# Other homes for the second branch's turned blocks in a decoder block, and another split of the first branch's transfers over two queues

## The chip, the cores and the metric

The kernel runs on one core of one Trainium2 chip. The metric is the device time of one execution in microseconds (us); before the change the median of three runs is 363.88 us (363.3 to 364.21). Engines are named as in the profile: PE (TensorE), DVE (VectorE), ACT (ScalarE), POOL (GpSimd) and SP (SyncE, which here issues transfers and nothing else). Each engine runs its own instructions in order, and so do the queues into which SP and POOL issue transfers: an instruction that waits holds up all that stand behind it on its engine.

## What is computed

One decoder layer on a sequence of 256 positions with 1024 channels. Two attention branches of 8 heads with 64 channels run side by side on the normalised input; their outputs are gated channel by channel, added and projected, and a gated feed-forward part with a short causal convolution follows. Cut to what matters:

```python
h = rms_norm(x, attn_norm_g)
qa, ka, va, qb, kb, vb, f_logit, g_logit = split(h @ w_in)
qa, ka = partial_rope(rms_norm(heads(qa))), partial_rope(rms_norm(heads(ka)))   # first branch
qb, kb = rms_norm(heads(qb)), rms_norm(heads(kb))                               # second branch
o_a = softmax(mask(qa @ ka.T / 8)) @ va          # one block of 256 keys: causal attention
c   = cumsum(log_sigmoid(f_logit + b_forget))
o_b = softmax(mask(qb @ kb.T / 8 + c[t] - c[s])) @ vb
merged = sigmoid(g0) * (o_a @ w_moba) + sigmoid(g1) * (o_b @ w_fox)
x = x + merged @ w_out
u, g = split(rms_norm(x) @ w_up)
x = x + (silu(conv3(g)) * u) @ w_down
```

All of it is float32 with float32 weights, 66.75 MB of which are read from device memory.

## The kernel before

**Weights.** Every weight chunk is 1 MB (128 x 2048). SP issues its load into one of three buffers "raw" (L132). ACT splits each half into a rounded high part (whi, L141) and DVE into the rest (wlo, L142), six buffers of each; a product is then three matmuls, high by high, high by low and low by high. So every chunk costs two ACT and two DVE instructions, and a raw buffer comes free, and with it the next load, when DVE has taken the second half. The chunks are used in the order of the list `chunks`: q and k of the second branch, `qkv` 1 and 2; gate chunks `wg` 0 and 1; V of the first branch, `qkv` 0 in the halves (0,0) and (0,1); `wg` 2; V of the second branch, `qkv` 3; `wg` 3 to 7; and then the later matrices. q and k of the first branch come with the input in the chunks called "head".

**q and k.** Products of q and k come out with positions on the partitions, and attention wants channels there. `finish_qk` normalises them into qns[0] (tag "qn", first branch) or qns[1] (tag "ol", second branch); in the first branch POOL then applies the rotation in place (L357 to L360). `turn_blocks` (L370) turns them in blocks of 32 x 32 with two DVE transposes of 1024 columns, first the half d=1 and then d=0 (L375), into the tile "pT". `move_blocks` (L380) carries the blocks to their partitions with sixteen transfers of 64 KB (L385), eight on SP for d=1 and eight on POOL for d=0, into the tile "bias". ACT then copies them, scaled, to qTs and kTs (L393 and L396), five instructions in each branch; the second branch's lie in the space "oh".

**Shared space.** "pT" and "bias" have one buffer each, and both branches use them. The second branch's turn into pT therefore waits for the first branch's sixteen transfers out of it, and the second branch's transfers into bias wait for ACT's copies of the first. V (128 x 2 x 1024) is written by `finish_v` (L321, L323) only after the first softmax; "qn" is free from the first branch's turn until the second softmax takes it for two pairs of heads (L497); "bias" becomes the second branch's bias (`forget_bias`, L448), and both pT and bias later take turned probabilities (`turn`, L530).

**Order.** PE's order is the program's. For the other engines a planner picks the order by priorities and expected times, within the orders that `after` writes out by hand. Those that touch this change: SP's transfers of a branch come after a load given as `behind` (L388: `qkv` (0,0) for the first branch, (0,1) for the second); the load of `qkv` (0,1) comes after the first branch's last SP transfer, and that of `wg` 2 after the second's (L134, through `sent_last`); the second branch's turn comes after the split of `wg` 1 (L377, `state["turn"]`); the forget gate's sums (`forget_a`, L408) come after that turn; ACT's split of `qkv` (0,1) comes after its copies of the first branch (L149, `moved[0]`), and the first softmax's exponentials after its copies of the second (L511, `moved[1]`).

PE meanwhile runs: q and k of the second branch, gates 0 and 1, scores of the first branch (L481), V of the first branch (L317), gate 2, scores of the second branch (L481), V of the second branch, gates 3 to 7, and so on.

Of the kernel before, what the change touches and what calls it, by code (L numbers as in the profile page):

```python
# [17 lines left out]
P = 128  # L18
# [26 lines left out]
def decoder_block(ctx, tc, a, out):  # L45
    nc = tc.nc
# [6 lines left out]
    def T(shape, tag, bufs=1, dt=F32):  # L53
        return sb.tile(shape, dt, tag=tag, bufs=bufs, name=tag)
# [4 lines left out]
    def bank():  # L59
        return ps.tile([P, 512], F32, tag="bank", bufs=8, name="bank")  # L60
# [36 lines left out]
    moved = []  # L97
    sent_last = []
# [3 lines left out]
    def after(i, j):  # L102
        tc.add_manual_dep(i.ins, j.ins.name, mybir.DependencyInfo(mybir.DependencyClass.NoSync, mybir.DependencyReason.DATA), reason="order")
# [85 lines left out]
    def col(c, n=1):  # L189
        return sm[:, c:c + n]  # L190
# [104 lines left out]
    V = T([P, NT, 2 * W4], "V")  # L295
# [73 lines left out]

    def turn_blocks(br, behind):  # L370

        blocks = T([P, 3072], "pT")
        for d in (1, 0):
            c = slice(d * 1024, (d + 1) * 1024)
            i = nc.vector.transpose(blocks[:, c], qns[br][:, c])  # L375
            if br or d == 0:
                after(i, behind)  # L377
        return blocks, i

    def move_blocks(br, blocks, behind):  # L380
        moved = T([P, 3072], "bias")
        for d, queue in ((1, nc.sync), (0, nc.gpsimd)):
            for h in range(2):
                for a in range(4):
                    sent = queue.dma_start(moved[64 * h + 32 * d:64 * h + 32 * (d + 1), a * 512:(a + 1) * 512],  # L385
                                           blocks[32 * a:32 * (a + 1), (2 * d + h) * 512:(2 * d + h + 1) * 512])
                    if d:
                        after(sent, behind)  # L388
            if d:
                sent_last.append(sent)  # L390
        v = moved[:, 0:2048].rearrange("p (a s b t i) -> p s t b a i", a=4, s=2, b=4, t=NT)
        q = moved[:, 0:2048].rearrange("p (a s g i) -> p s g a i", a=4, s=2, g=8)[:, 0]
        i = nc.scalar.activation(qTs[br].rearrange("p b (t a i) -> p (b t) a i", t=NT, a=4), q, AF.Copy, scale=gq[:, br:br + 1])  # L393
        kT = kTs[br].rearrange("p b (n a i) -> p n b a i", n=4, a=2)
        for t, a, at in ((0, 0, 2), (0, 2, 3), (1, 0, 1), (1, 2, 0)):
            i = nc.scalar.activation(kT[:, at], v[:, 1, t, :, a:a + 2], AF.Copy, scale=col(C_QG + 2 * br + 1))  # L396
        return i
# [230 lines left out]
    for isk in range(2):  # L628
        pt = banks()
        state["lag"] = 2 * isk  # L630
        project(3 + isk, pt, 0)
        project(3 + isk, pt, 1)
        with soon(FIRST):
            finish_qk(1, ((isk, pt),))
            if isk == 0:
                blocks, i = turn_blocks(0, state["qn"])
# [3 lines left out]
    with soon():  # L640
        moved.append(move_blocks(0, blocks, loads["qkv", 0, 0]))
        blocks, i = turn_blocks(1, state["turn"])
        summed = forget_a(i)
        after(state["v_lo"], summed)
# [4 lines left out]
    with soon():  # L649
        sps = scores(0, read)  # L650
        moved.append(move_blocks(1, blocks, loads["qkv", 0, 1]))
        for pair in range(4):
            scaled = softmax(0, pair, sps[pair], read, moved[1])
            if pair == 0:
                done = scaled
# [93 lines left out]
    sp = bank()  # L749
# [141 lines left out]
```

## Time and profile before

| | us |
|---|---|
| median of three runs | 363.88 |
| the profiled execution | 365.09 |
| its span (first to last instruction) | 363.3 |
| PE busy | 353.3 |
| DVE busy | 278.4 |
| ACT busy | 221.8 |
| POOL busy | 47.7 |

The profile is of one execution. Its own time is 1.8 us more than its span; what the kernel's instructions do lies within the span. Lines of the profile's groups read: line, engine, operation, tile written <- tiles read, count, busy time and mean, and the idle time of that engine just before, with what ended it. In lines in order of time the first two numbers are the start and the time taken in us; "x8" is a run of eight instructions; brackets hold the idle time before and what ended it. For a transfer the time is that of its issue on SP or POOL; when its data has landed is told apart.

### The profile page before, as it was taken

How to read it: one execution, taken by the hardware profiler on the slowest of the kernel's cores; microseconds unless marked ns; L12 is line 12 of the kernel's file. 1: busy time of each engine (PE TensorE's matmuls, PEld its weight loads, DVE VectorE, ACT ScalarE, POOL GpSimd, SP SyncE). 2: the span in 40 equal slices, each digit the busy share in tenths (PEclk: the TensorE clock that was granted, in tenths of full speed). 3: DMA queues.
4: the chain of work that ended last, by engine and by line, in shares of the span. 5: the costliest groups of instructions: out<-in, count | busy, mean ns of one | idle time of the engine just before them, and what ended most of it. 6: DMA issues, size and time to landing. Idle time of an engine off the chain costs nothing.

```text
span 363.3 us, 7518 instructions
## 1 busy us (share of the span) xinstructions
PE 353.3 (97%) x3053; PEld 335.9 (92%) x3053; DVE 278.4 (77%) x476; ACT 221.8 (61%) x378; POOL 47.7 (13%) x73
## 2 busy tenths in 40 slices
PE   9999999898889999999999999999999999999995
PEld 5888898697689999999999999999999999999995
DVE  4899997987998457984979876768686866768643
ACT  5859635499993998544778545546455545546420
POOL 2542751360050000000530000000000000000000
PEclk9999999999999999999999999999999999999998
DMA  7976483767238273654545754554554554554003
GB/s 276 403 307 240 130 252 105 248 267 293 108 116 325 75 299 117 234 197 159 225 145 204 231 195 160 227 189 166 226 187 173 221 203 160 219 191 157 3 0 117
DMA packets 13411, 70.39 MB, mean 194 GB/s; under 512 B 2200, under 2 KB 3360, under 8 KB 5952
## 3 DMA queue, kind: packets, MB, share of 16 engines
q1 hardware_dynamic: 12432, 67.67, 51.7%
q0 software_dynamic: 800, 2.24, 1.9%
q8 instruction: 24, 0.39, 0.4%
q14 instruction: 11, 0.09, 0.1%
q10 hardware_dynamic: 144, 0.00, 0.0%
HBM read 66.75 MB, written 1.06 MB: 187 GB/s over the span
## 4 chain that ended last, share of the span: by engine, by line
PE 72%; DVE 9%; ACT 6%; DMA 5%; SPq 3%; issue 2%; POOL 1%; DVEq 0%; ACTq 0%
PE bank L592 13%; PE bank L590 13%; PE bank L591 13%; PE bank L805 6%; PE bank L804 5%; PE bank L803 5%; DVE wlo L142 3%; PE bank L317 3%; ACT whi L141 2%; PE bank L727 2%; PE bank L701 2%; PE bank L729 2%; PE bank L728 2%; PE bank L703 2%; PE bank L702 2%
## 5 line engine op out<-in xcount | busy, mean ns | idle before, releaser
L142 DVE TENSOR_TENSOR wlo<-raw,whi 128x1024 fp32r<-128x1024 f32 x120 | 146.7, 1229 | 46.7 <-ACT whi L141 46.6
L141 ACT ACTIVATE whi<-raw 128x1024 fp32r<-128x1024 f32 x120 | 125.2, 1058 | 63.1 <-PE bank L591 37.1
L592 PE MATMUL bank<-oh,wlo 128*128 128x256 f32 x352 | 96.8, 275 | 0.0
L590 PE MATMUL bank<-oh,whi 128*128 128x256 f32 x352 | 96.8, 275 | 0.0
L591 PE MATMUL bank<-ol,whi 128*128 128x256 f32 x352 | 96.8, 275 | 0.0
L592 PEld LDWEIGHTS bank<-oh,wlo 128*128 128x128 f32 x352 | 66.1, 188 | 0.0
L590 PEld LDWEIGHTS bank<-oh,whi 128*128 128x128 f32 x352 | 66.1, 188 | 0.0
L591 PEld LDWEIGHTS bank<-ol,whi 128*128 128x128 f32 x352 | 66.1, 188 | 0.0
L590 PE MATMUL bank<-xh,whi 128*128 128x256 f32 x128 | 35.7, 279 | 1.5 <-ACT ol L509 1.5
L592 PE MATMUL bank<-xh,wlo 128*128 128x256 f32 x128 | 35.4, 276 | 1.3 <-DVE wlo L142 1.3
L591 PE MATMUL bank<-xl,whi 128*128 128x256 f32 x128 | 35.3, 276 | 0.0
L590 PEld LDWEIGHTS bank<-xh,whi 128*128 128x128 f32 x128 | 24.0, 188 | 2.5 <-ACT ol L509 1.9
L592 PEld LDWEIGHTS bank<-xh,wlo 128*128 128x128 f32 x128 | 24.0, 188 | 1.5 <-DVE wlo L142 1.5
L591 PEld LDWEIGHTS bank<-xl,whi 128*128 128x128 f32 x128 | 24.0, 188 | 0.1
L317 PE MATMUL bank<-wlo,xh 128*128 128x512 f32 x64 | 21.1, 390 | 1.1 <-DVE wlo L142 1.1
L317 PE MATMUL bank<-whi,xh 128*128 128x512 f32 x64 | 21.2, 391 | 0.1
L317 PE MATMUL bank<-whi,xl 128*128 128x512 f32 x64 | 20.9, 388 | 0.0
L770 DVE TENSOR_TENSOR sq<-bank,rs 128x512 f32<-128x512 f32 x22 | 15.1, 691 | 6.6 <-PE bank L592 6.5
L701 PE MATMUL bank<-oh,whi 128*128 128x256 f32 x64 | 17.6, 275 | 0.0
L702 PE MATMUL bank<-ol,whi 128*128 128x256 f32 x64 | 17.6, 275 | 0.0
L703 PE MATMUL bank<-oh,wlo 128*128 128x256 f32 x64 | 17.6, 275 | 0.0
L727 PE MATMUL bank<-xh,whi 128*128 128x256 f32 x64 | 17.6, 275 | 0.0
(196 smaller groups left out, 767.0 us busy)
## 6 DMA issues: line engine op xcount, KB each, us to landing
raw<-in_wu SPq DMA_DIRECT2D x22, 1024.0 KB, 4.8
raw<-in_wd SPq DMA_DIRECT2D x11, 1024.0 KB, 4.8
raw<-in_qkv SPq DMA_DIRECT2D x8, 1024.0 KB, 6.3
raw<-in_wg SPq DMA_DIRECT2D x8, 1024.0 KB, 4.9
raw<-in_wb SPq DMA_DIRECT2D x4, 1024.0 KB, 5.1
raw<-in_wo SPq DMA_DIRECT2D x4, 1024.0 KB, 4.9
raw<-in_head SPq DMA_DIRECT2D x6, 512.0 KB, 6.6
bias<-pT SPq DMA_DIRECT2D x16, 64.0 KB, 3.7
```

What stands on the lines that cost most here:

```text
L141: i = nc.scalar.activation(hi[:, s], raw[:, s], AF.Copy)
L142: d = nc.vector.tensor_tensor(lo[:, s], raw[:, s], hi[:, s].bitcast(F32), op=ALU.subtract)
L317: nc.tensor.matmul(pt[t], lhs[:, k, t * P:(t + 1) * P], rhs[:, c], start=(k == 0 and i == 0), stop=(k == KT - 1 and i == 2))
L590: nc.tensor.matmul(o, wh[:, w], mh[:, k], start=(k == 0 and i == 0), stop=False)
L591: nc.tensor.matmul(o, wh[:, w], ml[:, k], start=False, stop=False)
L592: nc.tensor.matmul(o, wl[:, w], mh[:, k], start=False, stop=(k == KT - 1 and i == 1))
L701: nc.tensor.matmul(o, wh[:, w], oh[:, 4 * br + k], start=(k == 0), stop=False)
L702: nc.tensor.matmul(o, wh[:, w], ol[:, 4 * br + k], start=False, stop=False)
L703: nc.tensor.matmul(o, wl[:, w], oh[:, 4 * br + k], start=False, stop=(k == 3))
L727: nc.tensor.matmul(o, wh[:, w], mh[:, k], start=(k == 0 and i == 0), stop=False)
L803: nc.tensor.matmul(o, wh[:, w], ah, start=(p == 0 and h == 0 and c == 0), stop=False)
L805: nc.tensor.matmul(o, wl[:, w], ah, start=False, stop=(last and h == 1 and d == ds[-1]))
```

## The change

Three things are changed, all within `turn_blocks` and `move_blocks`:

- the second branch's blocks are turned into V's tile, seen as 128 x 2048, instead of into pT;
- they are carried into a tile of the tag "qn" (128 x 2048) instead of "bias";
- the first branch's sixteen transfers are split twelve to four: the eight of d=1 and the four of d=0 with h=0 on SP, the four of d=0 with h=1 on POOL. The second branch's stay eight and eight. What the load of the next chunk is put behind (`sent_last`) is still the branch's last transfer on SP.

```diff
     def turn_blocks(br, behind):
 
-        blocks = T([P, 3072], "pT")
+        blocks = V.rearrange("p t c -> p (t c)") if br else T([P, 3072], "pT")
         for d in (1, 0):
             c = slice(d * 1024, (d + 1) * 1024)
             i = nc.vector.transpose(blocks[:, c], qns[br][:, c])
@@
     def move_blocks(br, blocks, behind):
-        moved = T([P, 3072], "bias")
-        for d, queue in ((1, nc.sync), (0, nc.gpsimd)):
+        moved = T([P, 2048], "qn") if br else T([P, 3072], "bias")
+        for d in (1, 0):
             for h in range(2):
+                sp = d or h < 1 - br
+                queue = nc.sync if sp else nc.gpsimd
                 for a in range(4):
                     sent = queue.dma_start(moved[64 * h + 32 * d:64 * h + 32 * (d + 1), a * 512:(a + 1) * 512],
                                            blocks[32 * a:32 * (a + 1), (2 * d + h) * 512:(2 * d + h + 1) * 512])
-                    if d:
+                    if sp:
                         after(sent, behind)
-            if d:
-                sent_last.append(sent)
+                if sp:
+                    last = sent
+        sent_last.append(last)
```

## The prediction

> **What bounds the kernel now.** I read the page first (busy times, then the slices), then TensorE's waits and time order, then the chain of waits, then the time order of each queue between 40 and 110 us. Busy times, and TensorE's share of 40 equal slices of the span (9 is 90% or more):
>
> ```profile
> PE 353.3 (97%) x3053; PEld 335.9 (92%) x3053; DVE 278.4 (77%) x476; ACT 221.8 (61%) x378; POOL 47.7 (13%) x73
> PE   9999999898889999999999999999999999999995
> ```
>
> TensorE is busy nearly always; what it loses is four stalls in the middle (in brackets, with what ended each; columns are start us, us, what):
>
> ```profile
> 65.68 0.50 PE L317 MATMUL bank<-wlo,xh 128*128 128x512 f32 x1 [1.13 <-DVE wlo L142]
> 84.31 1.31 PE L481 MATMUL bank<-oh 64*64 64x64 f32 x30 [1.12 <-ACT V L321]
> 98.39 0.36 PE L590 MATMUL bank<-xh,whi 128*128 128x256 f32 x1 [1.53 <-ACT ol L509]
> 108.37 0.38 PE L592 MATMUL bank<-xh,wlo 128*128 128x256 f32 x1 [1.31 <-DVE wlo L142]
> ```
>
> They are 5.1 us in all, the most that an edit of this stage can win. After the last, at 108.37 (the twelfth slice), every slice but the final one is full, so a lead won before 108 reaches the end unchanged.
>
> What do they hang on? The chain of waits (start, us, what) has, ahead of the first softmax:
>
> ```profile
> 52.62 6.40 DMA bias<-pT
> ...
> 62.69 1.70 SPq L385
> ...
> 67.69 4.97 DMA raw<-in_wg
> ...
> 72.75 1.06 ACT whi L141
> ```
>
> and ScalarE (ACT), asked for its waits from 72 to 110 us, has one only:
>
> ```profile
> ACT whi L141 <- DMA raw<-in_wg: 0.5, 1, 0.5
> ```
>
> So ScalarE works without a gap from 72.75 to 110, beginning with the split of gate chunk 2. The chunk's load is issued at 67.69, because SP's queue is in order and the eight transfers of the second branch's q and k stand in front of it; these stood waiting for the first branch. VectorE (DVE) has small gaps in 73 to 100 us, each ended by ScalarE. The second, third and fourth stall follow this pair of engines; the first follows VectorE alone.
>
> **The change part by part.**
>
> *Second branch turned into V's space.* VectorE, in time order:
>
> ```profile
> 55.78 1.22 DVE L142 TENSOR_TENSOR wlo<-raw,whi 128x1024 fp32r<-128x1024 f32 x1
> 59.30 2.37 DVE L375 STREAM_TRANSPOSE pT<-ol 128x1024 f32<-128x1024 f32 x2 [2.31 <-DMA bias<-pT]
> 63.36 0.41 DVE L417 TENSOR_TENSOR gates<-gates,rsB 8x256 f32<-8x256 f32 x1
> 63.80 0.69 DVE L600 TENSOR_TENSOR gates<-bank,rsB 128x512 f32<-128x512 f32 x1
> 64.41 3.49 DVE L142 TENSOR_TENSOR wlo<-raw,whi 128x1024 fp32r<-128x1024 f32 x3
> 70.55 0.27 DVE L427 TENSOR_SCALAR gates<-gates 8x256 f32<-8x256 f32 x1
> 73.85 1.23 DVE L142 TENSOR_TENSOR wlo<-raw,whi 128x1024 fp32r<-128x1024 f32 x1 [1.11 <-ACT whi L141]
> ```
>
> The turn waits 2.31 us until the first branch's transfers have left pT. V isn't written before 83.59 (below), so the wait goes: turns from 57.0 to 59.3, the first half done at 58.2. All that follows moves 2.3 up as far as its inputs allow. L417 ends at 61.4; L600 needs the second gate's last product (TensorE goes on to L481 at 61.48, a row below), so it starts at about 61.6 and 0.1 is lost there; the three splits run from 62.2 to 65.7. The first is done at 63.4, and TensorE comes for it at 64.5: the stall of 1.13 goes. L427 comes at 68.3, and VectorE stands at the split of chunk 2, for which it is free at about 72.7 now, at 70.5.
>
> *Second branch carried into qn's space.* SP and GpSimd (POOL) queues:
>
> ```profile
> 44.23 5.83 SPq L385 DMA_DIRECT2D bias<-pT  x8
> 50.16 1.49 SPq L132 DMA_DIRECT2D raw<-in_qkv  x1
> 61.50 6.15 SPq L385 DMA_DIRECT2D bias<-pT  x8
> ```
> ```profile
> 49.13 3.99 POOL L385 DMA_DIRECT2D bias<-pT  x8 [3.14 <-DVE pT L375]
> 62.20 1.47 POOL L385 DMA_DIRECT2D bias<-pT  x3 [9.09 <-DVE gates L414]
> 63.85 2.44 POOL L385 DMA_DIRECT2D bias<-pT  x5 [0.18 <-issue]
> ```
>
> Now SP may begin only when ScalarE has read the first branch out of bias (61.47). In qn's space the last readers are the first branch's turns, over before 49.13, when GpSimd, which waits for them, begins; so SP waits for the first half's turn alone, and begins at 58.2 instead of 61.50. Its eight issues took 6.15, with one of 1.70 among issues of 0.6; without that one, about 5.1. I take 6.15: SP is through at 64.4, the load of chunk 2 is issued there instead of at 67.69, and lands 4.97 later, at 69.4. GpSimd begins some 0.5 after the second turn (62.20 against 61.67), at 59.8, and ends at 63.9, where it ended at 66.3.
>
> ScalarE, in time order:
>
> ```profile
> 58.72 0.91 ACT L396 ACTIVATE kT<-bias,sm 128x256 f32<-128x256 f32 x2 [5.75 <-DMA bias<-pT]
> 60.58 0.89 ACT L396 ACTIVATE kT<-bias,sm 128x256 f32<-128x256 f32 x2
> 61.38 1.99 ACT L141 ACTIVATE whi<-raw 128x1024 fp32r<-128x1024 f32 x2
> 68.73 0.91 ACT L396 ACTIVATE oh<-bias,sm 128x256 f32<-128x256 f32 x2 [3.97 <-DMA bias<-pT]
> 71.82 0.42 ACT L429 ACTIVATE gates<-gates 8x256 f32<-8x256 f32 x1
> 72.75 1.06 ACT L141 ACTIVATE whi<-raw 128x1024 fp32r<-128x1024 f32 x1 [0.52 <-DMA raw<-in_wg]
> 83.59 0.67 ACT L321 ACTIVATE V<-bank,rsw 128x512 f32<-128x512 f32 x1
> ```
>
> It began to read the second branch 1.1 after SP's last issue ended (67.65 to 68.73) and took 2.75. So: 65.5 to 68.2, then L428 and L429, which need L427, to 69.3. Chunk 2 has landed at 69.4; its split starts at 69.5, not 72.75: **3.25 us** earlier. VectorE, free at 70.5, follows when that split is done, at 70.6, not 73.85. Both engines enter the softmax 3.2 ahead with the same work in the same order.
>
> *New waits.* V's first writer (L321, some 80.4 then) waits for sixteen transfers landed by 67: 13 us of cover. The second softmax's writes to qn's space near 100 us wait for reads over at 68. Nothing is late by these.
>
> *First branch, twelve on SP and four on GpSimd.* The chain's 6.40 is GpSimd's last transfer of that branch, issued beside the 1 MB load of 50.16. Four of GpSimd's eight go: its part ends at 51.1 instead of 53.1. SP gets four more, behind its eight that end at 50.06, when the turns are done: 4 x 0.6 = 2.4, up to 3.5 with one slow issue. The load behind them goes out at 52.5 to 53.6 instead of 50.16.
>
> ```profile
> raw<-in_qkv SPq DMA_DIRECT2D x1, 1024.0 KB, 8.4
> bias<-pT SPq DMA_DIRECT2D x16, 64.0 KB, 3.7
> ```
>
> By these rows (KB each, us from issue to landing) that load landed at 58.5 and will at about 59 to 61; it is split from 61.38 now, and its first VectorE half is due at 64.5, so that is covered. The first branch lands at 53.0 + 3.7 = 56.7, not 59.0, and ScalarE has read it by 59.2, not 61.47. TensorE wants it at 61.48:
>
> ```profile
> 61.48 2.41 PE L481 MATMUL bank<-kT,qT 64*64 64x64 f32 x64
> ```
>
> Value: 0 to 0.1 us, since the second branch no longer waits for the first. I take 0. At worst, with the load at 61 and split to 63, still 0; at best 0.1.
>
> **The sum.** TensorE's stalls: the first (1.13) and second (1.12) fall away, 2.25; the third is set by engines 3.2 ahead, so 0.95 of its 1.53 goes; the fourth keeps its length, as TensorE and VectorE are then equally far ahead. Together 3.2 us. The profiled execution took 365.09, of which 363.3 is span: it would take 361.9. Against the median of the runs, 363.88, which I predict: **360.7**. Bounds: below, VectorE's own 2.3 if ScalarE's order gives nothing beyond it; above, 3.6 if SP's slow issue doesn't recur (VectorE then limits), and the 5.1 of all stalls if the planner also reorders.
>
> **A rule against it.** GpSimd's tensor operations can be held by VectorE here:
>
> ```profile
> 38.96 0.46 POOL L358 TENSOR_TENSOR p<-qn,rsn 128x128 f32<-128x128 f32 x1
> 42.57 1.51 POOL L358 TENSOR_TENSOR p<-qn,rsn 128x128 f32<-128x128 f32 x1
> 42.55 1.21 DVE L142 TENSOR_TENSOR wlo<-raw,whi 128x1024 fp32r<-128x1024 f32 x1
> ```
>
> 1.51 instead of 0.46, beside a split of weights. Its transfer issues were not: 0.49 each, beside splits too (3.99 for eight, 2.44 for five). The Trainium skill (SBUF — State Buffer, "SBUF: two separate sides") says that a transfer issued from GpSimd can starve, since VectorE in some modes locks GpSimd out of the port through which it writes descriptors. By that rule the second branch's last issues, now at 62 to 64 with splits from 62.2 to 65.7 beside them, would be held; the rows speak against it. The rival that it gives is the third below.
>
> **The rivals.**
> 1. *One transfer is caught by the load.* The first branch's fifth to eighth GpSimd transfers, issued from 0.5 us before the load's issue ended (51.65), landed late; the last took 6.40. Here the last is issued at 63.4, the load's issue (0.6) ends at 65.0, 1.6 later, which is safe; if SP has no slow issue it ends at 63.9, and the last transfer may land at 68 to 68.5. ScalarE then reads until 70.8, and its split starts at 71.6: 1.2 won, 362.7. Between, 2 won.
> 2. *The planner puts the work elsewhere.* ScalarE's copies of the second branch, or the turns, keep their old place or stand behind something late; only the first stall's 1.1, or nothing, is won, as ScalarE sets the rest: 363.2 (362.8 to 364.2).
> 3. *GpSimd is held by the splits.* From 62.2 the last three issues wait until 65.7 and end at 67.1, in the midst of 1 MB loads; with 6.40 to landing, 73.0 to 73.5, ScalarE has read them at 75.9 rather than 71.47, so its chain is 4.2 later: 368.1. It decides from the point where the last landing passes 69.1, that is an issue after 62.7 that is caught. For it: nothing but the 1.51 above; against it: every issue at 0.49.
> 4. *More than the sum*: all of the third and part of the fourth stall go too, 359.6.
>
> **Chances.** Forecast (360.0 to 361.6) 0.57; rival 1 0.13; rival 2 0.15; rival 3 and other losses 0.08; rival 4 0.07. 0.3% of 363.88 is 1.1 us, about what a measurement of this kernel can tell from no change. Faster by more: 0.57 + 0.07 + 0.11 of rival 1 = 0.75; within: 0.17; slower: 0.08. The range leaves out the far ends: 359.8 to 363.2.
>
> **What would show it.** Right: the turns L375 without a wait behind the split at about 57; SP's second group of L385 from 58.2; the load of chunk 2 issued near 64.4; ScalarE's split of it near 69.5; no stall of L317 and L481, a third of 0.6 and a fourth of about 1.3. Wrong: L375 or L385 still waiting for a transfer or for ScalarE; GpSimd's issues further apart than 0.5; second-branch landings after 67; or VectorE idle before the first softmax; or a stall after 110 us that isn't there now.

## The result, and the profile after

The changed kernel took 361.97 us in the median of its runs (361.6 to 362.1), against 364.04 for the kernel before in the same comparison: a ratio of 0.9945 (95% interval 0.9928 to 0.9962). Two later comparisons gave 0.9958 and 0.9952 (below). So the change gains 1.6 to 2.1 us; the forecast was 3.2, and 360.0 to 361.6 as the range of its main case. The profiled execution took 361.60, of which 359.8 is span.

Lines from `move_blocks` on are numbered 2 or 3 higher than before: L385 is now L387, L393/L396 are L396/L399, L481 is L484, L590/L592 are L593/L595, L427 to L429 are L430 to L432, L505/L509 are L508/L512, L600 is L603. (Experiments e7 to e9 add two lines more.) First the busy times, and TensorE in 40 slices of the span:

```profile
PE 352.3 (98%) x3053; PEld 335.1 (93%) x3053; DVE 278.4 (77%) x476; ACT 221.7 (62%) x378; POOL 44.6 (12%) x69
PE   9999999999889999999999999999999999999995
```

The work is the same, but for the four issues that went from GpSimd to SP; the dip in the middle is narrower. Asked for its waits, TensorE has two left of four, here in order of time:

```profile
95.16 0.36 PE L593 MATMUL bank<-xh,whi 128*128 128x256 f32 x1 [1.53 <-ACT ol L512]
105.14 0.38 PE L595 MATMUL bank<-xh,wlo 128*128 128x256 f32 x1 [1.32 <-DVE wlo L142]
```

The stall at V of the first branch (1.13) and that at V of the second (1.12) are gone. The third, which was to shrink to 0.6, is what it was. Next the queues of SP and POOL (start, us of issue, what):

```profile
43.70 9.35 SPq L387 DMA_DIRECT2D bias<-pT  x12
53.16 0.52 SPq L132 DMA_DIRECT2D raw<-in_qkv  x1
57.69 4.96 SPq L387 DMA_DIRECT2D qn<-V  x8
62.75 0.89 SPq L132 DMA_DIRECT2D raw<-in_wg  x1
```
```profile
48.62 2.05 POOL L387 DMA_DIRECT2D bias<-pT  x4 [3.15 <-DVE pT L375]
59.30 3.92 POOL L387 DMA_DIRECT2D qn<-V  x8 [8.64 <-DVE gates L417]
```

The second branch's transfers begin at 57.69, as soon as the first turn is done, and the load of gate chunk 2 goes out at 62.75. VectorE and ScalarE, in order of time:

```profile
56.39 2.37 DVE L375 STREAM_TRANSPOSE V<-ol 128x1024 f32<-128x1024 f32 x2
61.05 0.69 DVE L603 TENSOR_TENSOR gates<-bank,rsB 128x512 f32<-128x512 f32 x1 [0.19 <-PE bank L595]
67.80 0.27 DVE L430 TENSOR_SCALAR gates<-gates 8x256 f32<-8x256 f32 x1
```
```profile
53.44 0.91 ACT L399 ACTIVATE kT<-bias,sm 128x256 f32<-128x256 f32 x2 [0.99 <-DMA bias<-pT]
61.31 1.99 ACT L141 ACTIVATE whi<-raw 128x1024 fp32r<-128x1024 f32 x2
66.03 0.91 ACT L399 ACTIVATE oh<-qn,sm 128x256 f32<-128x256 f32 x2 [2.43 <-DMA qn<-V]
68.10 0.42 ACT L431 ACTIVATE gates<-gates 8x256 f32<-8x256 f32 x1
69.53 0.39 ACT L512 ACTIVATE s<-s,nm 128x128 f32<-128x128 f32 x1
70.41 1.04 ACT L141 ACTIVATE whi<-raw 128x1024 fp32r<-128x1024 f32 x1
```

The turn L375 has no bracket: its wait of 2.31 is gone. ScalarE reads the first branch from 53.44 instead of 58.72 and the second from 66.03 instead of 68.73; from there it has no gap up to 110 us. The planner has also changed ScalarE's order: the forget gate's exponentials L431 and L432 now stand between the last copies, and four instructions of the softmax (69.53 to 70.41) ahead of the split of chunk 2. Without them that split would stand at 69.53, 3.22 before its old place of 72.75.

The chain of waits no longer passes a transfer here:

```profile
60.90 0.13 PE bank L595
...
61.66 3.49 DVE wlo L142 x3
...
66.76 1.12 DVE wlo L142
67.88 0.20 DVE gates L430
...
68.10 0.42 ACT gates L431
68.52 0.40 ACT oh L399
68.92 0.31 ACT gates L432
```

It runs from the last product of gate 1 (60.90) over VectorE to the forget gate's exponential L431. Yet this is a near tie: ScalarE came free from the first three of its five copies of the second branch at 68.04 (66.88 + 1.16), and L430 ended at 68.07.

**A second profile of the kernel before.** The forecast worked from one execution, of 365.09. Another of the same kernel (363.90, span 362.1) gives:

```profile
58.36 2.37 DVE L375 STREAM_TRANSPOSE pT<-ol 128x1024 f32<-128x1024 f32 x2 [1.80 <-DMA bias<-pT]
64.75 0.50 PE L317 MATMUL bank<-wlo,xh 128*128 128x512 f32 x1 [0.65 <-DVE wlo L142]
83.12 1.31 PE L481 MATMUL bank<-oh 64*64 64x64 f32 x30 [0.84 <-ACT V L321]
```

The wait and the first two stalls are shorter (1.80, 0.65, 0.84) than in the execution that the prediction used (2.31, 1.13, 1.12). Against this one, the changed kernel's matmuls start at the same times, to 0.1 us, up to the first stall (they are 0.09 earlier just before it); from there they are 0.90 to 1.04 earlier (63.85 for 64.75), from the second stall on 2.05 earlier (81.07 for 83.12), and the third and fourth stalls are alike in both. Net of the 0.09 the change won 1.97 here; the medians of the three comparisons have 2.1, 1.6 and 1.8. Against the profile used in the prediction the lead at the same place is 3.24, of which 0.53 was there at 12 us already, from the arrival of the first loads, which the change doesn't touch; net 2.71.

### The profile page after: what moved, and what is told of

Read it like the earlier page. It is cut to its first block, busy times and chain, and to the rows that moved or that the text cites. A ratio compares the mean times of both kernels' runs of the same rounds, so it can differ in the third digit from the quotient of the medians.

```text
span 359.8 us, 7495 instructions
## 1 busy us (share of the span) xinstructions
PE 352.3 (98%) x3053; PEld 335.1 (93%) x3053; DVE 278.4 (77%) x476; ACT 221.7 (62%) x378; POOL 44.6 (12%) x69
## 3 DMA queue, kind: packets, MB, share of 16 engines
HBM read 66.75 MB, written 1.06 MB: 188 GB/s over the span
## 4 chain that ended last, share of the span: by engine, by line
PE 90%; ACT 5%; DVE 4%; issue 1%; DVEq 0%
PE bank L593 14%; PE bank L595 14%; PE bank L594 14%; PE bank L317 9%; PE bank L303 6%; PE bank L807 6%; PE bank L806 6%; PE bank L808 6%; PE bank L732 2%; PE bank L706 2%; DVE wlo L142 2%; PE bank L731 2%; PE bank L730 2%; PE bank L705 2%; PE bank L704 2%; ACT s L512 2%
## 5 line engine op out<-in xcount | busy, mean ns | idle before, releaser
L595 PE MATMUL bank<-oh,wlo 128*128 128x256 f32 x352 | 96.8, 275 | 0.0
L593 PE MATMUL bank<-oh,whi 128*128 128x256 f32 x352 | 96.8, 275 | 0.0
L593 PEld LDWEIGHTS bank<-oh,whi 128*128 128x128 f32 x352 | 66.1, 188 | 0.0
L595 PEld LDWEIGHTS bank<-oh,wlo 128*128 128x128 f32 x352 | 66.1, 188 | 0.0
L593 PE MATMUL bank<-xh,whi 128*128 128x256 f32 x128 | 35.7, 279 | 1.5 <-ACT ol L512 1.5
L595 PE MATMUL bank<-xh,wlo 128*128 128x256 f32 x128 | 35.4, 276 | 1.3 <-DVE wlo L142 1.3
L593 PEld LDWEIGHTS bank<-xh,whi 128*128 128x128 f32 x128 | 24.0, 188 | 2.6 <-ACT ol L512 1.9
L595 PEld LDWEIGHTS bank<-xh,wlo 128*128 128x128 f32 x128 | 24.0, 188 | 1.5 <-DVE wlo L142 1.5
```

The source lines that it names most:

```text
L593: nc.tensor.matmul(o, wh[:, w], mh[:, k], start=(k == 0 and i == 0), stop=False)
L595: nc.tensor.matmul(o, wl[:, w], mh[:, k], start=False, stop=(k == KT - 1 and i == 1))
```

## The experiments

Two theories were set against each other. **One: a single chain of waits with two cures.** The second branch has to wait for the first one's transfers to leave pT and bias. Other spaces remove the wait; landing the first branch sooner (twelve transfers on SP) ends it in time. Either should do, and both together no more than one. **The prediction's:** the spaces bring the gain, and the split is worth 0 to 0.1. The kernels with a part undone keep the rest of the changed kernel. Each ratio is to the kernel before, run on the same chip in the same comparison.

**The changed kernel and the kernel before again** (no edit): a0_after and a1_after are the changed kernel beside other experiments, b0_before the kernel before.

> The changed kernel again, for a narrower interval and a second profile. Theory one (the second branch's landing sets the start of the softmax): ratio 0.993 to 0.996, ScalarE begins to read the second branch near 66 us and from there works without a gap; two stalls of TensorE left, 1.5 and 1.3 us. Rival (the 3.5 us between the two profiled spans is the change): ratio 0.990 or below.

> The changed kernel beside the three above, for comparison on the same chip: 361.9 +- 0.4.

> The kernel before, timed against itself, for the width of the measurement and a second profile of it. Theory three (the first profiled execution was a slow one: its first branch landed at 59.0 where those of e1, e4 and e6 landed at 57.5 to 57.9): ratio 1.000 +- 0.002, first branch landed by 58, VectorE's wait ahead of the second branch's turn near 1.2 rather than 2.3, span near 362. Rival: 59.0 and 2.3 again.

Measured: a0_after 361.92 against 363.54 (0.9958, 0.9943 to 0.9974); a1_after 361.88 against 363.65 (0.9952, 0.9936 to 0.9968); b0_before 363.92 against 363.38 (1.0004, 0.9992 to 1.0017). Both profiles of the changed kernel have TensorE's two stalls of 1.5 and 1.3 and no others. b0_before's profile is the second profile of before shown above.

**Spaces without the split** (e1_spaces):

```diff
-                sp = d or h < 1 - br
+                sp = d
```

> Only the two spaces (V and qn); the first branch's transfers stay eight and eight. Theory one, either cure is enough: the first branch lands at 59 again, ScalarE has copied it by 61.5, but the second branch's turn (57) and transfers (58) don't wait for that; the time is that of the whole change, 362.0 +- 0.4. Rival, the split of the transfers is what counts: 363.9 +- 0.4.

Measured: 362.61 against 363.54 (0.9979, 0.9964 to 0.9994), about half the gain.

**The split without the spaces** (e2_split):

```diff
-        blocks = V.rearrange("p t c -> p (t c)") if br else T([P, 3072], "pT")
+        blocks = T([P, 3072], "pT")
...
-        moved = T([P, 2048], "qn") if br else T([P, 3072], "bias")
+        moved = T([P, 3072], "bias")
```

> Only the split twelve to four; pT and bias shared as before. Theory one, either cure is enough: the first branch lands at 54.5, its copies are over at 56.5, so the second branch's turn finds pT free at 57 and its transfers find bias free at 58; the time is that of the whole change, 362.0 +- 0.4. Rival, which is what the prediction's step says (the split is worth 0 to 0.1, the spaces carry the gain): 363.8 to 364.0.

Measured: 362.08 against 363.54 (0.9957, 0.994 to 0.9973): the whole gain of the change, from the part that the prediction valued at 0 to 0.1. Its DVE, SP and ACT in order of time:

```profile
56.87 2.36 DVE L375 STREAM_TRANSPOSE pT<-ol 128x1024 f32<-128x1024 f32 x2
```
```profile
58.19 4.96 SPq L387 DMA_DIRECT2D bias<-pT  x8
```
```profile
56.49 0.89 ACT L399 ACTIVATE kT<-bias,sm 128x256 f32<-128x256 f32 x2
59.38 2.01 ACT L141 ACTIVATE whi<-raw 128x1024 fp32r<-128x1024 f32 x2 [2.00 <-DMA raw<-in_qkv]
66.38 0.91 ACT L399 ACTIVATE oh<-bias,sm 128x256 f32<-128x256 f32 x2 [4.05 <-DMA bias<-pT]
```

The turn goes into pT, which the first branch still had to leave, and doesn't wait: its transfers have all landed at 55.3. SP writes into bias at 58.19, when ScalarE is through with it (57.38). All engines but SP and GpSimd work in the same order here as in the kernel before, up to 100 us, so the planner has no part in this gain. The price is seen on ACT: the load of `qkv` (0,1), now behind twelve transfers, holds up its split by 2.00; that is covered, as TensorE has only the two stalls of 1.5 and 1.3.

Why does the first branch land so much sooner? The trace gives for each GpSimd transfer of that branch the time from issue to the landing of its last piece. A few kernels:

```
                  issue of load       GpSimd transfers    from issue to      first branch
                  qkv (0,1) ends      issued after ~ it   landing, these     landed
before            51.65               4 (from 51.16)      5.2 to 7.1         59.0
e1_spaces         50.78               5 (from 50.48)      5.4 to 6.6         57.9
e3_v_only         49.95               6 (from 49.77)      6.6 to 8.0         58.9
e8_qn_order       51.69               2 (from 51.68)      5.2 to 5.5         57.3
after             53.68               none                (2.8 to 3.6)       54.4
```

Small transfers that GpSimd issues from about half a microsecond before the end of the 1 MB load's issue take 5 to 8 us, those before it 2.6 to 4. With four on GpSimd, all are out by 50.7 and the load follows at 53.16: none is caught. The split does two things at once, it takes four transfers from GpSimd and it sends the load 3 us later; no run has one without the other.

**One space alone** (e3_v_only: V for the turn, bias kept, 8/8; e4_qn_only: qn for the transfers, pT kept, 8/8; the edits are the lines above, one each, with `sp = d`).

> V's space alone: turn into V, transfers into bias, eight and eight. The turn of the second branch starts at 57 without its 2.3 us wait, but SP still begins the second branch after ScalarE's copies of the first, at 61.5. Theory one (ScalarE's start after the second branch sets the end): TensorE's first stall of 1.1 goes, and comes back in the later ones; 363.9 +- 0.4. Rival (VectorE's 2.3 us earlier work carries the gain): 362.0 to 362.8.

> qn's space alone: turn into pT, transfers into qn, eight and eight. The second branch's turn waits until the first branch's last transfer has left pT (59.0), then SP begins at 60.5 instead of 61.5. Theory one (the end follows ScalarE's start on the second branch): that start comes 1.0 earlier, near 67.7, and the time is 362.6 to 363.0, ratio 0.997 to 0.998; TensorE's first stall of 1.1 stays. Rival (this space carries the change): 362.0.

Measured: e3_v_only 363.34 against 363.54 (0.9991, 0.998 to 1.0002), nothing; e4_qn_only 364.48 against 363.65 (1.0018, 1.0004 to 1.0032), a little slower than before, where 362.6 to 363.0 was expected. In e3 the turn is early, but SP and ACT stand where they did before:

```profile
68.23 0.91 ACT L399 ACTIVATE oh<-bias,sm 128x256 f32<-128x256 f32 x2 [4.06 <-DMA bias<-V]
```

In e4 the turn still waits 1.19 for pT (1.80 and 2.31 in the two profiles of the kernel before), and SP begins the second branch at 59.22 (60.56 and 61.50); that should still have been a gain. What it lost is an order of the planner. Waits of all engines of e4_qn_only from 66 to 78 us (engine, line, what it waited for: us in total, times, longest), and its ACT in order of time:

```profile
DVE cW L438 <- POOL gates L437: 1.2, 1, 1.2
...
ACT s L512 <- DVE nm L508: 0.7, 2, 0.5
```
```profile
70.67 1.06 ACT L141 ACTIVATE whi<-raw 128x1024 fp32r<-128x1024 f32 x1 [0.54 <-DMA raw<-in_wg]
71.63 0.40 ACT L432 ACTIVATE gates<-gates 8x256 f32<-8x256 f32 x1
```

The split of chunk 2 stands ahead of the last forget exponential L432 and waits for its data. GpSimd's forget products wait for L432, VectorE's scan L438 for GpSimd, and ScalarE's softmax for VectorE. e1_spaces has the same order (whi at 69.36 after 0.50 of waiting, L432 at 70.32) and the same waits; the changed kernel, e2 and before have L432 first.

**The same with that order put right** (e7_spaces_order is e1, e8_qn_order is e4, each with):

```diff
+                if (c, h) == (("wg", 2), 0):
+                    after(i, state["fr"])
...
-        nc.scalar.activation(r, l, AF.Exp, scale=-1.0)
+        state["fr"] = nc.scalar.activation(r, l, AF.Exp, scale=-1.0)
```

> The two spaces alone, as e1_spaces, with one order by hand: ScalarE's split of chunk 2 behind its last exponential of the forget chain. Theory four (e1's shortfall against the whole change is the planner's order: the split stood ahead of that exponential, so that VectorE's scan waited 1.2 for GpSimd and ScalarE stood still for 1.5 in all): 361.9 +- 0.4, as the whole change. Rival (the split twelve to four gives the missing 0.7 itself): 362.6 again.

> qn's space alone, as e4_qn_only, with the same order by hand. Theory four: the 0.8 by which e4 was slower than the kernel before goes, and the time is 362.6 to 363.2. Rival (this space costs something): 364.4 again.

Measured: e7_spaces_order 361.69 against 363.38 (0.995, 0.9931 to 0.9968), e8_qn_order 363.17 against 363.38 (0.9988, 0.9975 to 1.0001). So the order cost e1 and e4 about 1 us each (0.9979 to 0.995, and 1.0018 to 0.9988). Up to the third stall it shows in TensorE's waits (those of 55 to 125 us, in the form above): e7 has one of 1.1 there, e1 has these two:

```profile
PE bank L593 <- ACT ol L512: 1.7, 1, 1.7
PE bank L484 <- ACT V L321: 0.6, 1, 0.6
```

With the order written out the planner also places two later splits of ScalarE anew (at 80.0 and 105.3 in e1, at 79.0 and 102.2 in e7), so a part of that 1 us may be theirs; the second lies behind the third stall, and the fourth is 1.3 in both. With the order put right, the spaces alone, with a first branch that lands as late as 58.9, give what the whole change gives. ACT and PE of e7:

```profile
65.19 0.91 ACT L401 ACTIVATE oh<-qn,sm 128x256 f32<-128x256 f32 x2 [1.02 <-DMA qn<-V]
68.28 0.42 ACT L433 ACTIVATE gates<-gates 8x256 f32<-8x256 f32 x1 [0.34 <-DVE gates L432]
69.05 1.05 ACT L141 ACTIVATE whi<-raw 128x1024 fp32r<-128x1024 f32 x1
```
```profile
94.79 0.36 PE L595 MATMUL bank<-xh,whi 128*128 128x256 f32 x1 [1.06 <-ACT ol L514]
```

Here the third stall did shrink, from 1.53 to 1.06. In this kernel all five copies of the second branch stand ahead of the two forget exponentials (L433 and L434 in its numbering).

**What keeps ScalarE from reading the second branch at 65?** In the changed kernel its first six transfers land 1.9 to 2.1 us after issue, and the last eight 3.9 to 4.2; of those eight, fifteen DMA engines are through by 65.2 and one only at 66.65. That lag begins with a 16 KB fetch of instructions, seen among the queues of the changed kernel from 61.9 to 66.8 us (packets, MB, share of 16 engines):

```profile
q8 instruction: 1, 0.02, 1.3%
```

The packet starts at 62.34 and takes 0.99. Such packets are most likely TensorE's instructions: every profile here has 24 of them, and between the first and the last TensorE runs 254 to 256 matmuls and weight loads for each. To move it, e5_after_warm takes the changed kernel, and e6_before_warm the kernel before, with 68 short warm-up matmuls instead of 9 long ones; nothing reads what they write.

```diff
-NWARM = 9
+NWARM = 68
...
-        nc.tensor.matmul(wp, warm[:, 0:P], warm, start=True, stop=True)
+        nc.tensor.matmul(wp[:, 0:64], warm[:, 0:P], warm[:, 0:64], start=True, stop=True)
```

> The changed kernel with 68 warm-up products of 64 columns instead of 9 of 512, which moves TensorE's 16 KB instruction fetches earlier against its work by some half of their distance. Theory two (one DMA engine, busy with such a fetch near 62.5, lands its share of the second branch's last ten transfers 1.3 late): the fetch near 62.5 goes to about 56, these transfers land within 2.5 us of issue on all engines, ScalarE begins on the second branch near 65.0; 0.3 to 0.7 faster than the changed kernel, no more, since VectorE then limits. Rival (that engine is late for another cause, as the load of chunk 2 behind them): the last landing stays at about 66.6.

> The kernel before with the same 68 short warm-up products. Theory two: SP's one slow issue of 1.7 in the second branch goes, the second branch lands up to 1 us sooner; the first branch's transfers caught by the load stay late, 6 us and more from issue. Time 363.0 to 363.9. Rival (warm-up products change the start, by the clock or by the order): the products of the first chunks run later or slower and all is shifted.

Measured: the fetch moves to 56.8 and 56.5; all engines' orders stay those of the changed kernel and the kernel before. In e5 all of the second branch lands within 3.1 us of its issue, on every engine, by 65.90. The time doesn't follow: 361.83 against 363.65 (0.9942, 0.9922 to 0.9962), where a1_after had 361.88 in the same comparison. ACT of e5:

```profile
64.92 0.91 ACT L399 ACTIVATE oh<-qn,sm 128x256 f32<-128x256 f32 x2 [1.25 <-DMA qn<-V]
66.13 1.16 ACT L396 ACTIVATE oh<-qn,gq 128x1024 f32<-128x1024 f32 x1 [0.29 <-issue]
68.18 0.42 ACT L431 ACTIVATE gates<-gates 8x256 f32<-8x256 f32 x1 [0.90 <-DVE gates L430]
68.50 0.49 ACT L399 ACTIVATE oh<-qn,sm 128x256 f32<-128x256 f32 x1
```

ScalarE begins 1.1 earlier and then waits 0.90 for VectorE's L430, with a copy that could have filled the wait standing behind it. e6 gained somewhat more than expected: 362.83 against 363.65 (0.997, 0.9957 to 0.9984); its first branch landed at 57.46, its second could be read from 65.94, and the turn waited 0.93. Its first branch was still caught beside the load: the GpSimd transfer issued at 50.48 landed at 56.40, 5.9 later and before the fetch at 56.5, so that lateness isn't the fetch's. The same move of the fetch is thus worth something in the kernel before and nothing that could be measured in the changed kernel.

**Is it VectorE's own work that is late?** e9_warm_copy is e5 with the first copy of the forget sums on ACT:

```diff
-        after(nc.vector.tensor_copy(total, fp[0:NH, :S]), behind)
+        nc.scalar.activation(total, fp[0:NH, :S], AF.Copy)
...
```

(The order `behind` goes to the first of VectorE's additions instead; those lines are left out here.)

> The changed kernel with the short warm-up products of e5 and the first copy of the forget sums on ScalarE, which is idle then, instead of VectorE. Theory five (with the second branch landed early VectorE limits the entry into the softmax): VectorE's 0.4 less comes out, 361.4 to 361.6, and ScalarE's wait for L430 shrinks from 0.9 to 0.5. Rival (something else limits): 361.8 to 361.9 as e5.

Measured: 361.93 against 363.38 (0.9951, 0.9938 to 0.9964); the 361.4 to 361.6 that was expected isn't there. DVE and ACT:

```profile
61.18 0.69 DVE L605 TENSOR_TENSOR gates<-bank,rsB 128x512 f32<-128x512 f32 x1 [0.56 <-PE bank L597]
```
```profile
68.24 0.42 ACT L433 ACTIVATE gates<-gates 8x256 f32<-8x256 f32 x1 [1.01 <-DVE gates L432]
```

What VectorE saves it spends waiting for gate 1's last product, and everything behind stays: L605 at 61.18, where the changed kernel has it at 61.05. So VectorE's entry into this stage is set by TensorE itself.

## Why the prediction was right in direction and too large

- **The turn's wait (2.31) goes, nothing is late in its place**: right. L375 runs without a wait; L603 waits 0.19 for gate 1's product, as the 0.1 of the prediction had it. No new wait on V's or qn's space appeared.
- **SP from 58.2, chunk 2 issued at 64.4**: right. It was 57.69 and 62.75; in the time of the profile used, which ran 0.53 later from 12 us on, 58.22 and 63.28. The load went out 1.1 earlier than forecast because SP's slow issue did not fall among its eight (4.96 instead of 6.15).
- **ScalarE reads the second branch from 65.5**: off. In the time of the profile used it was 66.03 + 0.53 = 66.56. The term "1.1 after SP's last issue" came from an execution in which SP's last issue was itself late, and hid what sets the reading: one DMA engine that runs 1.2 to 1.6 behind the other fifteen after the fetch. Half of the 1.06 was covered, since the forecast let ScalarE wait for L427 anyway.
- **The split of chunk 2 at 69.5, 3.25 earlier**: 3.22 by the clock, but 2.7 once the 0.53 of an earlier start, which TensorE has too, is taken off. Nor does the load of chunk 2 bind any more: it lands at 68.8, and its split comes at 70.41.
- **The first and the second stall, 2.25 together**: right that both go. In that profile TensorE's net lead was 2.71 and not 2.25, since a stall costs more than the idle time in its bracket: 1.13 of idle held the matmuls behind it back by 1.41 and 1.12 by 1.30, and in the second profile of before 0.65 by 0.95 and 0.84 by 1.02 (the ends of matmuls are modelled, and the first one after the stall is slower, 0.34 us from start to start, then 0.24). There the two stalls are worth 1.97.
- **The third stall loses 0.95**: this is the step that failed. It rests on engines 3.2 ahead and TensorE 2.25 ahead; they were 2.7 and 2.7 ahead, so the stall stayed at 1.53. Both leads were mis-sized: that of the engines by the late reading and by the 0.53, that of TensorE by taking the brackets for the cost of the stalls.
- **12/4 is worth 0 to 0.1, "since the second branch no longer waits for the first"**: true beside the spaces (e7 has all the gain without the split), but the reason cuts both ways: beside the split, the spaces are worth nothing that could be measured (e2). Taken alone, the split gives 1.5. So this step failed too: it let the spaces act first and gave the split what was left. Theory one held, with one addition: the spaces alone need the last forget exponential ahead of the split of chunk 2 on ScalarE, which the planner doesn't choose in e1 and does in the changed kernel.
- **The sum and the median.** 3.2 − 0.95 (third stall) + 0.46 (2.71 for 2.25) = 2.71, the net lead over the profile used. Against the second profile it is 1.97, because its two stalls are shorter (1.49 of idle together, not 2.25), with an earlier landing of the first branch (58.08, not 59.02). The prediction took the stalls from an execution of 365.09 and subtracted them from a median of 363.88. This adds up what the profiles show and doesn't test it: two executions of the kernel before are few, and the medians' 1.6 to 2.1 leave room.
- **The number.** 361.97 lies above the main case's 360.0 to 361.6 and within the full range. It is close to the first rival's "between, 2 won", but by luck: what that rival rests on, a transfer of the second branch caught by the load, did not happen.
- **The rivals.** One transfer caught by the load: not here, GpSimd's last issue was at 62.73 and the load's ended at 63.64, and no transfer took over 4.2. But the same effect is what the split cures in the first branch. The planner's order: it did change in the changed kernel, against the prediction's "same work in the same order", but e2, with the order of before, took as long (362.08, 361.92 for the changed kernel beside it), so it cost nothing that could be measured; it took about 1 us of the gain in e1 and in e4. GpSimd held by the splits: no, eight issues took 3.92 with the three splits beside the later ones; the Trainium skill's rule (SBUF — State Buffer, "SBUF: two separate sides") that VectorE in some modes keeps GpSimd from writing its transfers' descriptors did not show in this trace, at 0.49 for each. The prediction applied that rule to these splits without a row that shows them in such a mode, and no run here shows one. More than the sum: only e7's third stall moved that way, by 0.5.

**What stays open.** ScalarE's two copies behind L431 cost e5 and e9 a wait that those copies could fill, and e7, where they stand ahead and the reading begins at 65.19, has the shorter third stall (e2, with the same order but a reading from 66.38, has 1.5). Whether e5 with that order would be faster than the changed kernel wasn't tried. Of the kernels that were, e5, e7, e9 and the changed kernel lie within 0.3 us, less than the runs can tell apart. Whether the load sent later, with eight transfers left on GpSimd, would do what the split does, wasn't tried either; and why transfers beside a load's issue land late, no run says.

## What to carry to other kernels

Where an engine waits for a shared buffer, look for both cures, another space and an earlier release; one can make the other worthless, so try each alone before paying for both. Here four small transfers moved from GpSimd to SP, ahead of a large load in its queue, were worth as much as two changes of space (1.5 us): look whether small transfers land late beside a large load. Read stalls from more than one execution before subtracting them from a median, and let a stall shrink in a forecast only by the difference of the two leads that make it.

## What the runs showed of the hardware beyond that

- **A fetch of instructions delays one DMA engine's share of what follows.** A single 16 KB packet (0.99 us in the changed kernel, 1.60 in e2) was followed by one of sixteen shares coming 1.2 to 2.1 us behind the others for the next eight transfers of 64 KB, and each counts as landed only with its last share. It isn't always as much: in e7, with a fetch of 1.08 at 62.79, the last five transfers were 0.5 to 0.8 behind. With the fetch elsewhere (e5) no share was more than 0.2 behind, and the same transfers landed in at most 3.1 us instead of 4.2.
- **SP's slow issues come with it.** In the profile used for the prediction SP took 1.70 for the issue at 62.69, beside a fetch at 62.55; in e6 with the fetch moved its eight took 4.96, none above 0.60. In the changed kernel and e2 it is the load of chunk 2, issued at that time, that took 0.89 and 1.71 instead of 0.53. In all eleven profiles with a fetch at 62.3 to 63.1 one of these nine issues of SP took 0.9 to 1.9; in the three with the fetch moved (e5, e6, e9) none took more than 0.60.
- **What GpSimd issues beside a 1 MB load of SP lands late**, 5 to 8 us after issue instead of 2.1 to 4.1, if issued from about half a microsecond before the end of the load's issue on (the first branch's transfers; some in the table above), in every kernel of this study that has eight transfers there and in none that has four.
